# Writes of the gate tables and loads of the expert inputs moved from SyncE's DMA queue to ScalarE's

## The chip, the cores and the metric

The kernel runs on one core of a Trainium2 chip. The metric is the device time of one execution in microseconds (us): 3339.67 us before the change, the median of 3 runs (3336.93 to 3353.06).

## The reference, cut to what matters

One layer of a decoder, for 1024 prompt positions and 8 x 4 sample positions (1056 tokens, D = 1024): a mixing stage (RWKV-7 heads and pooling heads), then a layer of product-key experts, then a gate by a per-layer embedding and a final norm. The expert layer picks 8 x 16 of 16384 single-neuron experts for each token:

```python
q = (xb @ wq).reshape(PEER_BLOCK, PEER_HEADS, 2, PEER_DK_HALF)
s1 = jnp.einsum('thc,nc->thn', q[:, :, 0], sub_keys[0])
s2 = jnp.einsum('thc,nc->thn', q[:, :, 1], sub_keys[1])
v1, i1 = lax.top_k(s1, PEER_TOPK)
v2, i2 = lax.top_k(s2, PEER_TOPK)
cand = (v1[..., :, None] + v2[..., None, :])
sc, ci = lax.top_k(cand.reshape(...), PEER_TOPK)
expert = e1 * N_KEYS + e2
gate = jax.nn.softmax(sc)
act = gelu(einsum('thkd,td->thk', u_tab[expert], xb)) * gate
out = einsum('thk,thkd->td', act, v_tab[expert])
```

## The kernel before, in words

The work is one long program of unrolled instructions. A planner orders it: it takes the instructions as the code emits them, with their dependencies, and places them on the five engines by a model of their times. Each engine runs its own list in order. Almost every DMA is issued by SyncE (SP); the row gathers are issued by GpSimd (POOL). ScalarE (ACT) issues none.

Stages: `phase_a` projects and prepares the RWKV rows (0 to about 550 us). Then the tokens go in four groups (GROUPS, 288, 256, 256 and 256 tokens) through three streams that `merge` interleaves (lines 1124 to 1140): `b_stream` (the RWKV recurrence in chunks of 64 positions), `phase_c` (output projection, norm, query projection, key scores: its weights come as `whi`/`wlo` loads of 256 KB in `wblock`, lines 646 and 647, three buffers each), and `t_stream` (for the 672 tokens of positions GA to GB: top-k and gate tables, in `top` and `select`). Its scores go through memory as `sc_d` (written at line 747, read back at line 762).

The gate tables: for these 672 tokens the expert layer is computed densely, over all 16384 experts. `select` builds for 32 tokens at a time a table `gst` of 128 x 128 gates per token, as products of one-hot masks: VectorE and GpSimd build the masks `ab` (lines 898 to 900), TensorE multiplies them into PSUM (line 903), ScalarE copies the result into `gst` (line 905, 8 copies a table, 128 x 512 each), and the finished table (2 MB) is written to the memory tensor `g_d` (line 907). `gst` has two buffers. There are 21 such tables. `ugate` reads `g_d` back later, 32 loads `gq` of 1344 KB each, at line 1164.

The expert inputs: `phase_c` writes the normalised rows of the 672 tokens, split in two parts for precision, to `xh_d` and `xl_d` (line 719). When three of the four steps are emitted, the buffers of the recurrence are given up, and `XH` and `XL` are loaded into their place in 2 x 8 loads of 336 KB (lines 1148 and 1149). The dense stage (`dense`, `ublock`, `vblock`, with the matmuls in `emm` at line 1110) multiplies them with all expert rows: `eraw` loads of 512 KB at line 1084, split by ScalarE (`ehi`, line 1086) and by VectorE or GpSimd (`elo`, line 1088). It begins with `upre` at about 1215 us and runs to about 3200 us. Tokens beyond GB are done by row gathers on GpSimd and VectorE (lines 1210 to 1250) beside it.

In the code a DMA's issuing engine is the one named in the call: `nc.sync.dma_start` is SyncE, `nc.scalar.dma_start` ScalarE.

Of the kernel before, what the change touches and what calls it, by code (L numbers as in the profile page):

```python
# [10 lines left out]
F32 = mybir.dt.float32  # L11
# [30 lines left out]
GA, GB = 0, 672  # L42
# [4 lines left out]
TC = 32  # L47
# [3 lines left out]
GQ = 4  # L51
# [11 lines left out]
def body(ctx, tc, io):  # L63
    nc = tc.nc
# [12 lines left out]
    xh_d = dram.tile([128, KB, ND], F32, name="xh_d")  # L77
    xl_d = dram.tile([128, KB, ND], F32, name="xl_d")
# [4 lines left out]
    g_d = dram.tile([EB // GQ, 128, NTC, GQ, TC], F32, name="g_d")  # L83

    def v3(ap, n):
        return ap.rearrange("p (a b) -> p a b", b=n)
# [40 lines left out]
    def PS(tag):  # L127
        return pools[tag].tile([128, 512], F32, name="ps", tag="bc" if tag in ("b0", "b1") else tag)
# [620 lines left out]
    def top(tk, pos, mt):  # L749
        src = sc_d[TIDX[pos]]  # L750
        if mt > TC:
            m, nh, loads = mt, HEADS, [(slice(0, mt), 0)]
        else:
            m, nh = mt * SH, HEADS // SH
            loads = [(slice(g * mt, (g + 1) * mt), 2 * nh * g) for g in range(SH)]
        V12 = tk.tile([128, HEADS, 2, TOPK], F32, name="V12", bufs=1)
        I12 = tk.tile([128, HEADS, 2, TOPK], U32, name="I12", bufs=1)
        for i in range(2 * nh):
            if i % 4 == 0:
                sq = tk.tile([128, 4, 128], F32, name="scq", bufs=2)  # L760
                for d, j in loads:
                    nc.sync.dma_start(sq[d], src[:mt, j + i:j + i + 4, :])
            s_ = sq[:m, i % 4, :]
            v8, i8 = V12[:m, i // 2, i % 2, :], I12[:m, i // 2, i % 2, :]
            nc.vector.max(v8[:, 0:8], s_)
            nc.vector.max_index(i8[:, 0:8], v8[:, 0:8], s_)  # L766
            s2 = tk.tile([128, 128], F32, name="s2", bufs=2)
            nc.vector.match_replace(s2[:m], v8[:, 0:8], s_, -BIG)  # L768
            nc.vector.max(v8[:, 8:16], s2[:m])
            nc.vector.max_index(i8[:, 8:16], v8[:, 8:16], s2[:m])  # L770
            yield
        yield from select(tk, pos, mt, m, nh, V12, I12)


    def select(tk, col, mt, m, nh, V12, I12):
# [6 lines left out]
        for src, dst, add in ((V12, cand, TT), (F12, code, PTT)):  # L782
            off = 0
            for a, b, w in SEG:
                k = b - a
# [101 lines left out]
        for t1 in range(0, m, TC):  # L887
            st = gp.tile([128, EB, TC], F32, name="gst", bufs=2)
            for t2 in range(0, TC, 4):
                ps = PS("b3")  # L890
                t = t1 + t2
                ab = gp.tile([128, 6, EB, 2], F16, name="ab", bufs=3)

                def pairs(j, n):
                    e = e16[:, t // 4, j:j + n // 2].rearrange("p j (a b) -> p (j a) b", b=2)
                    return e[:, :, None, :].to_broadcast([128, n, EB, 2])

                TT(ab[:, 0:4], iota16[:, None, :, :].to_broadcast([128, 4, EB, 2]), pairs(0, 4), op=ALU.is_equal)  # L898
                TT(ab[:, 4:6], ab[:, 2:4], pairs(2, 2), op=ALU.mult)  # L899
                GLO(t)(ab[:, 2:4], ab[:, 2:4], pairs(3, 2), op=ALU.mult)  # L900
                for i in range(4):
                    for k in (4, 2):
                        mm(ps[:, i * 128:(i + 1) * 128], ab[:, k + i // 2, :, i % 2], ab[:, i // 2, :, i % 2],  # L903
                           start=k == 4, stop=k == 2)
                ACT(st[:, :, t2:t2 + 4].rearrange("p e t -> p t e"), v3(ps, 128), AF.Copy, scale=1.0 / GS)  # L905
                yield
            nc.sync.dma_start(g_d[:, :, (col + t1 - GA) // TC].rearrange("g p e t -> p g e t"), st.rearrange("p (g e) t -> p g e t", e=GQ))

    NG = len(GROUPS)
    NSLOT = 3  # L910
# [4 lines left out]
    def b_stream(ca, cb, ahead=2):  # L915
        while nxt[0] < cb or any(c < cb for c, _ in active):
            c = nxt[0]
            if (c < min(cb + ahead, NCH) and len(active) < NSLOT and (not active or since[0] >= STAG)
                    and not (held[0] and c % NSLOT == 1)):
                active.append((c, bchunk(c)))  # L920
                nxt[0], since[0] = c + 1, 0
            since[0] += 1
            for a in list(active):
                try:
                    next(a[1])
                except StopIteration:
                    active.remove(a)
                yield

    def b_len(ca, cb):  # L930
        return (cb - ca) * 19
# [6 lines left out]
    def t_stream(gi):  # L938
        for t0, m in tiles_of(gi):
            if GA <= GROUPS[gi][0] + t0 < GB:  # L940
                yield from top(tk, GROUPS[gi][0] + t0, m)

    def t_len(gi):
        n = 0
        for t0, m in tiles_of(gi):
            if GA <= GROUPS[gi][0] + t0 < GB:
                n += 24 + m // 4
        return n

    def merge(streams):  # L950
        live = [[0, n, g] for n, g in streams]
        while live:
            s = min(live, key=lambda s: s[0] / s[1])
            try:
                next(s[2])
                s[0] += 1
            except StopIteration:
                live.remove(s)
# [109 lines left out]
    def GLO(t):  # L1068
        return PTT if t % 12 else TT

    def xsplit():
        return (dr.tile([128, KB, ND], F32R, name="XH"), dr.tile([128, KB, ND], F32R, name="XL"))
# [45 lines left out]
    def upre():  # L1118
        for b in range(NPRE):
            ublock(b, PTT)  # L1120
            yield

    CL = [0, 24, 24, 24, 24]
    for step in range(1, NG + 1):
        streams = []
        if step < NG:
            c_ = BC[step + 2:step + 4]
            streams.append((b_len(*c_), b_stream(*c_)))
        if 0 <= step - 2 < NG:
            streams.append((t_len(step - 2), t_stream(step - 2)))  # L1130
        if 0 <= step - 1 < NG:
            streams.append((CL[step], phase_c(step - 1)))
        if step == NG:
            for _ in streams[0][1]:
                pass
            gstack.close()
            late = ctx.enter_context(tc.tile_pool(name="late", bufs=1, side="right", reuse_waits="tile"))
            gqp = ctx.enter_context(tc.tile_pool(name="gqp", bufs=2, side="right", reuse_waits="tile"))
            streams = [streams[1], (NPRE, upre())]
        merge(streams)  # L1140
        if step == NG - 1:
            nc.sync.dma_start(io["wkv_p"], S[-1])
            pbx.close()
            dr = ctx.enter_context(tc.tile_pool(name="dr", bufs=1, side="right", reuse_waits="tile"))
            dps = ctx.enter_context(tc.tile_pool(name="dps", bufs=2, side="right", space=bass.MemoryType.PSUM, reuse_waits="tile"))
            XH, XL = xsplit()
            for k in range(KB):
                nc.sync.dma_start(XH[:, k, :].bitcast(F32), xh_d[:, k, :])
                nc.sync.dma_start(XL[:, k, :].bitcast(F32), xl_d[:, k, :])
            xs = [(XH[:, k, :], XL[:, k, :]) for k in range(KB)]  # L1150
    def gtop(col):
        for _ in top(tk, GB + col, min(128, GT - col)):
# [170 lines left out]
    XH, XL = xsplit()  # L1323
# [71 lines left out]
def program(arrays, extra=()):  # L1395
    nc = bacc.Bacc("TRN2", target_bir_lowering=False, num_devices=1)
    io = {k: nc.dram_tensor(k, v.shape, mybir.dt.from_np(v.dtype), kind="ExternalInput").ap()
          for k, v in arrays.items()}
    for k, s in list(OUTS.items()) + list(extra):
        io[k] = nc.dram_tensor(k, s, F32, kind="ExternalOutput").ap()  # L1400
    with tile.TileContext(nc, schedule_with_timeline_sim=True) as tc, ExitStack() as ctx:
        body(ctx, tc, io)
    return nc
# [15 lines left out]
```

## Time and profile before

| | |
|---|---|
| median of the runs | 3339.67 us (3336.93 to 3353.06, 3 runs) |
| the profiled execution, its own time | 3365.37 us |
| its span, first to last instruction | 3363.7 us |
| TensorE (PE) busy in the span | 3145.6 us, 94% |
| VectorE (DVE) | 2585.2 us, 77% |
| ScalarE (ACT) | 1128.8 us, 34% |
| GpSimd (POOL) | 1736.5 us, 52% |
| mean granted TensorE clock | 0.968 |
| DMA queue q1 (all issues of SyncE) | 337952 packets, 472.91 MB |
| DMA queue q0 (the row gathers) | 110592 packets, 402.70 MB |
| gate tables written | 21 x 2048 KB |
| `XH` and `XL` loaded | 16 x 336 KB |

How to read it: busy times are those of one profiled execution, whose own time is 0.8% above the median of the runs. A DMA issue is not counted as busy time of its engine. In the order of time of SP, the second column is the time that the issue took on the queue; the transfer itself goes on behind it. L907 is line 907 of the kernel.

### The profile page before, as it was taken

Reading aid. Unit: us, or ns where it says so; the run is one execution under the profiler, and the core shown is the slowest. Engines: PE = TensorE matmul, PEld = TensorE weight load, DVE = VectorE, ACT = ScalarE, POOL = GpSimd, SP = SyncE. Lnnn points to the kernel's source line nnn. Section 1 sums busy time; section 2 is a strip of 40 time slices with the busy share of each in tenths; the row PEclk is TensorE's granted clock in tenths of the full one; section 3 lists DMA queues with packets and bytes.
Section 4 is the critical chain, followed back from the end, with each engine's and each line's share of the span. In section 5 each row is a group of like instructions: output and inputs, shape, how many; then the busy total and the mean of one; then the engine's idle time right before and its main releaser. Section 6 shows DMA issues by size and latency. Waiting matters only on the chain.

```text
span 3363.7 us, 66962 instructions
## 1 busy us (share of the span) xinstructions
PE 3145.6 (94%) x26777; PEld 3006.4 (89%) x26777; DVE 2585.2 (77%) x5124; ACT 1128.8 (34%) x1734; POOL 1736.5 (52%) x1439
## 2 busy tenths in 40 slices
PE   8997799896998988899999999999999999999997
PEld 7886688786787877899999999999999999999997
DVE  6766322229799879899898888888889888888966
ACT  6452322223555555431221222222222222222243
POOL 5433232215446455327666665566566566666634
PEclk9998899997999989999999999999999999999998
DMA  4668544665776796739999999999999999999933
GB/s 160 203 219 195 145 130 127 204 191 149 235 217 201 232 317 204 244 109 371 343 330 332 343 349 328 333 334 339 337 336 349 326 330 342 338 329 337 323 107 127
DMA packets 448856, 879.89 MB, mean 262 GB/s; under 512 B 110240, under 2 KB 233376, under 8 KB 444064
## 3 DMA queue, kind: packets, MB, share of 16 engines
q1 hardware_dynamic: 337952, 472.91, 43.8%
q0 software_dynamic: 110592, 402.70, 32.9%
q8 instruction: 210, 3.44, 0.4%
q14 instruction: 102, 0.84, 0.1%
HBM read 754.89 MB, written 120.60 MB: 260 GB/s over the span
## 4 chain that ended last, share of the span: by engine, by line
PE 54%; DVE 7%; DMA 2%; issue 1%; ACT 0%; POOL 0%; SPq 0%; ACTq 0%; DVEq 0%; POOLq 0%
PE pd L1110 53%; DVE ab L898 1%; DMA row<-u,idx 1%; DVE elo L1088 1%; DVE oh L850 0%; DMA scq<-sc_d 0%; DMA eraw<-wq 0%; DVE OT L1316 0%; DVE ab L899 0%; DVE I L766 0%; DVE s L768 0%; DVE tg L1302 0%; DVE I L770 0%; DMA g_d<-gst 0%; DMA gq<-g_d 0%
## 5 line engine op out<-in xcount | busy, mean ns | idle before, releaser
L1219 POOL DMA_INDIRECT row<-v,idx x384 | 530.6, 1382 | 330.8 <-DVE po L1236 150.9
L1219 POOL DMA_INDIRECT row<-u,idx x384 | 542.5, 1413 | 274.9 <-DVE row L1227 107.4
L1086 ACT ACTIVATE ehi<-eraw 128x1024 fp32r<-128x1024 f32 x278 | 294.5, 1060 | 1095.9 <-PE pd L1110 976.8
L1110 PE MATMUL pd<-XH,elo 128*128 128x336 f32 x2176 | 515.3, 318 | 5.9 <-POOL elo L125 4.7
L1110 PE MATMUL pd<-XL,ehi 128*128 128x336 f32 x2176 | 515.1, 317 | 0.0
L1110 PE MATMUL pd<-XH,ehi 128*128 128x336 f32 x2176 | 512.4, 316 | 0.4 <-ACT ehi L1086 0.4
L1110 PE MATMUL pd<-wh,ehi 128*128 128x336 f32 (+1 forms) x2112 | 504.1, 317 | 6.6 <-DVE tg L1300 6.2
L1110 PE MATMUL pd<-wl,ehi 128*128 128x336 f32 (+1 forms) x2112 | 504.0, 317 | 0.0
L1110 PE MATMUL pd<-wh,elo 128*128 128x336 f32 (+1 forms) x2112 | 503.9, 317 | 0.2 <-DVE elo L1088 0.2
L1236 DVE SCALAR_TENSOR_TENSOR po<-row,act,po 128x1024 f32<-128x1024 f32 x381 | 488.5, 1282 | 6.8
L1227 DVE SCALAR_TENSOR_TENSOR row<-row,xt 128x1024 f32<-128x1024 f32 x384 | 455.7, 1219 | 9.7 <-DMA row<-u,idx 9.5
L1110 PEld LDWEIGHTS pd<-XH,elo 128*128 128x128 f32 x2176 | 373.5, 188 | 7.1 <-POOL elo L125 5.5
L1088 DVE TENSOR_TENSOR elo<-eraw,ehi 128x1024 fp32r<-128x1024 f32 x256 | 318.3, 1243 | 77.2 <-ACT ehi L1086 69.0
L1110 PEld LDWEIGHTS pd<-XH,ehi 128*128 128x128 f32 x2176 | 372.9, 189 | 0.9 <-ACT ehi L1086 0.6
L1110 PEld LDWEIGHTS pd<-XL,ehi 128*128 128x128 f32 x2176 | 371.3, 188 | 0.2
L1110 PEld LDWEIGHTS pd<-wh,ehi 128*128 128x128 f32 x2112 | 362.6, 188 | 7.6 <-issue 7.4
L1110 PEld LDWEIGHTS pd<-wh,elo 128*128 128x128 f32 x2112 | 362.7, 188 | 0.6 <-DVE elo L1088 0.5
L1110 PEld LDWEIGHTS pd<-wl,ehi 128*128 128x128 f32 x2112 | 362.8, 188 | 0.0
L125 POOL TENSOR_TENSOR ab<-ab,e 128x512 f16<-128x512 f16 x110 | 130.1, 1185 | 180.6 <-DVE ab L899 139.0
L657 PE MATMUL ps<-hi,whi 128*128 128x256 f32 (+1 forms) x592 | 185.7, 315 | 29.3 <-DMA whi<-wc_d 15.8
L1179 DVE TENSOR_TENSOR OT<-pd,OT 128x672 f32<-128x672 f32 x120 | 102.9, 857 | 140.7 <-PE pd L1110 139.8
L905 ACT ACTIVATE gst<-ps 128x512 f32<-128x512 f32 x168 | 174.9, 1089 | 85.5 <-PE ps L903 78.4
(428 smaller groups left out, 5526.9 us busy)
## 6 DMA issues: line engine op xcount, KB each, us to landing
eraw<-uT SPq DMA_DIRECT2D x128, 512.0 KB
eraw<-vP SPq DMA_DIRECT2D x128, 512.0 KB
g_d<-gst SPq DMA_DIRECT2D x21, 2048.0 KB
gq<-g_d SPq DMA_DIRECT2D x32, 1344.0 KB
whi<-wc_d SPq DMA_DIRECT2D x148, 256.0 KB
wlo<-wc_d SPq DMA_DIRECT2D x148, 256.0 KB
fdc<-fd SPq DMA_DIRECT2D x16, 896.0 KB
wc_d<-shi SPq DMA_DIRECT2D x40, 256.0 KB
```

Source lines behind the costliest of these rows:

```text
L125: nc.gpsimd.tensor_tensor(out, a, b, op=op)
L657: mm(ps[:, :n], whi[:, kk, :], xhi[:, k, :n], start=k == 0, stop=False)
L898: TT(ab[:, 0:4], iota16[:, None, :, :].to_broadcast([128, 4, EB, 2]), pairs(0, 4), op=ALU.is_equal)
L905: ACT(st[:, :, t2:t2 + 4].rearrange("p e t -> p t e"), v3(ps, 128), AF.Copy, scale=1.0 / GS)
L1086: ACT(hi, raw, AF.Copy)
L1088: sub(lo, raw, hi.bitcast(F32), op=ALU.subtract)
L1110: mm(ps[:, a, :n], w_[:, k, :], x_[:, s:s + n], start=first, stop=last)
L1179: TT(halves(OT[db]), ps[:, :, :NH], halves(OT[db]), op=ALU.add)
L1219: nc.gpsimd.indirect_dma_start(out=r[:m], out_offset=None, in_=io[tab], in_offset=bass.IndirectOffsetOnAxis(ap=idx[:m, hh, k:k + 1], axis=0))
L1227: STT(r[:m], r[:m], 1.0, xt[:m], op0=ALU.mult, op1=ALU.mult, accum_out=pre[:m, k:k + 1])
L1236: STT(po[:m], r[:m], act[:m, k:k + 1], po[:m], op0=ALU.mult, op1=ALU.add)
```

## The change

The 21 writes of the gate tables and the 16 loads of `XH` and `XL` are issued by ScalarE instead of SyncE. Nothing else differs: sizes, buffers and dependencies are the same.

```diff
-            nc.sync.dma_start(g_d[:, :, (col + t1 - GA) // TC].rearrange("g p e t -> p g e t"), st.rearrange("p (g e) t -> p g e t", e=GQ))
+            nc.scalar.dma_start(g_d[:, :, (col + t1 - GA) // TC].rearrange("g p e t -> p g e t"), st.rearrange("p (g e) t -> p g e t", e=GQ))
...
             for k in range(KB):
-                nc.sync.dma_start(XH[:, k, :].bitcast(F32), xh_d[:, k, :])
-                nc.sync.dma_start(XL[:, k, :].bitcast(F32), xl_d[:, k, :])
+                nc.scalar.dma_start(XH[:, k, :].bitcast(F32), xh_d[:, k, :])
+                nc.scalar.dma_start(XL[:, k, :].bitcast(F32), xl_d[:, k, :])
```

## Rows read from the trace of the kernel before

**Rows 1.** The chain that ended last, 1540 us to the end: start, us, what

```profile
1548.60 518.04 PE pd L1110 x3372
...
2643.67 560.14 PE pd L1110 x3644
```

**Rows 2.** Busy time of each engine by stage (clock, DMA share, GB/s last)

```profile
800.00:1400.00 600.00, 519.61 (x6117) 462.14 (x6113) 520.53 (x1971) 307.81 (x489) 300.55 (x311) 0.92 0.75 230
1400.00:1550.00 150.00, 147.65 (x963) 146.85 (x964) 134.08 (x546) 54.13 (x75) 52.67 (x57) 1.00 0.54 191
```

**Rows 3.** Waits of PE, 800 to 1400 us: us in total, times, longest

```profile
PE ps L903 <- DVE ab L899: 30.7, 21, 4.2
PE ps L657 <- DMA whi<-wc_d: 9.1, 7, 2.2
PE ps L903 <- ACT gst L905: 7.9, 14, 1.5
...
PE ps L659 <- DMA wlo<-wc_d: 1.4, 3, 0.8
```

**Rows 4.** Wait of DVE, 800 to 1400 us

```profile
DVE V L765 <- DMA scq<-sc_d: 7.6, 5, 3.6
```

**Rows 5.** SP in order of time: start, us of the issue, engine, line

```profile
835.74 0.37 SPq L907 DMA_DIRECT2D g_d<-gst  x1
836.20 5.95 SPq L647 DMA_DIRECT2D wlo<-wc_d  x1
...
856.33 3.42 SPq L907 DMA_DIRECT2D g_d<-gst  x1
...
1183.24 0.37 SPq L907 DMA_DIRECT2D g_d<-gst  x1
1183.85 8.97 SPq L646 DMA_DIRECT2D whi<-wc_d  x1
...
1207.43 0.38 SPq L907 DMA_DIRECT2D g_d<-gst  x1
1208.04 9.27 SPq L646 DMA_DIRECT2D whi<-wc_d  x1
...
1356.70 4.79 SPq L646 DMA_DIRECT2D whi<-wc_d  x1
```

**Rows 6.** PE in order of time, the larger waits for these loads (in brackets)

```profile
910.65 0.39 PE L657 MATMUL ps<-hi,whi 128*128 128x256 f32 x1 [0.54 <-DMA whi<-wc_d]
...
958.11 0.39 PE L657 MATMUL ps<-hi,whi 128*128 128x256 f32 x1 [1.07 <-DMA whi<-wc_d]
...
959.77 0.38 PE L659 MATMUL ps<-hi,wlo 128*128 128x256 f32 x1 [0.39 <-DMA wlo<-wc_d]
...
1094.19 0.38 PE L657 MATMUL ps<-hi,whi 128*128 128x256 f32 x1 [1.22 <-DMA whi<-wc_d]
...
1116.46 0.39 PE L659 MATMUL ps<-hi,wlo 128*128 128x256 f32 x1 [0.81 <-DMA wlo<-wc_d]
...
1157.50 0.58 PE L657 MATMUL ps<-hi,whi 128*128 128x256 f32 x1 [2.17 <-DMA whi<-wc_d]
```

**Rows 7.** PE's wait before the first dense block (order of time)

```profile
1221.01 0.93 PE L1110 MATMUL pd<-XH,elo 128*128 128x336 f32 x2 [4.68 <-POOL elo L125]
```

**Rows 8.** The issues of XH and XL: ns least, median, most; first and last start

```profile
L1148 SPq DMA_DIRECT2D XH<-xh_d x8: 319/372/653, 1176.3 to 1199.6; - x8
...
L1149 SPq DMA_DIRECT2D XL<-xl_d x8: 320/374/708, 1178.0 to 1200.5; - x8
```

**Rows 9.** The row gathers issued by POOL, ns least, median, most

```profile
L1219 POOL DMA_INDIRECT row<-u,idx x384: 932/1598/1992, 1507.2 to 3149.9; - x192
```

**Rows 10.** ACT, copies of L905 in 800 to 1400 us: busy, mean ns, idle before

```profile
L905 ACT ACTIVATE gst<-ps 128x512 f32<-128x512 f32 x168 | 174.9, 1089 | 85.5 <-PE ps L903 78.4 <-DMA g_d<-gst 5.3 <-ACT cF L827 0.4
```

**Rows 11.** The last table's write, in the chain of 1250 to 1560 us

```profile
1374.75 7.94 DMA g_d<-gst
...
1385.78 11.28 DMA eraw<-wq
```

## The prediction

> **What bounds the kernel now.** I read four views, in this order. First the chain of work that ended last: from 1548 us to the end it is TensorE's dense matmuls with hardly a break [rows 1]. Its three long pieces, the first of 518 us and the last of 560 us, need no explanation beyond TensorE itself, and none of the moved DMAs runs there. Whatever the change gives, it must give before 1548 us, by letting that chain start earlier, and what it gives there arrives at the end nearly whole, since the chain behind it is unbroken.
>
> Second, the busy time by stage. All 21 table writes and all 16 loads of XH and XL fall between 800 and 1400 us. There PE is busy for 519.6 of 600 us at a mean granted clock of 0.92, DVE for 520.5, ACT for 307.8 [rows 2]. So PE is idle for 80.4 us, and that is the pool from which a gain can be drawn. In the next 150 us PE is idle for 2.4 us, at full clock. DVE is as loaded as PE in the stage: a wait taken from PE may turn into a wait for DVE.
>
> Third, what PE waits for in these 600 us [rows 3]. The largest item is DVE's masks, 30.7 us, which the change doesn't touch. The weight loads of the projection (whi, wlo) cost 9.1 + 1.4 = 10.5 us in ten waits, ScalarE's copy of the table 7.9 us in 14.
>
> Fourth, SP in order of time [rows 5]. A table write itself takes 0.37 us on the queue. But the DMA issue behind it takes 5.95 us the first time, 4.79 us behind the second to last, against 0.37 us in the median for loads of a like size [rows 8]. I added up the next issue behind each of 20 of the 21 writes (the last has nothing close behind it): 108 us, from 1.7 to 9.3 us each; less 20 x 0.37 us that is about 100 us in which SP stands behind a table. That is what the change is aimed at, and the question is how little of it reaches PE.
>
> **The change part by part.**
>
> *The 21 writes leave SP.* The loads queued behind them no longer wait. Of the ten waits of PE for whi and wlo, six are for loads that stood behind a write: 0.54, 1.07, 0.39, 1.22, 0.81 and 2.17 us [rows 6], together 6.2 us. The other four, 10.5 - 6.2 = 4.3 us, have no table ahead of their load. The remaining 94 of the 100 us are hidden already: three buffers of weights are loaded ahead, and PE has other streams' matmuls to do. So this term is -6.2 us. Its ends: 0 if the loads are then just as late because the same 2 MB is moving beside them, and -10.5 us if all such waits go. I take 6.2, since a 256 KB load then has to share the transfer time with the table rather than stand behind the whole of it. The Trainium skill has a rule against this term (DMA: Bandwidth & Descriptors, Issuing engines are not separate DMA queues): DMAs from several engines end on the same 16 DMA engines, and issuing from more than one saves only the time of issuing, usually small beside the transfer. By that rule the term is 0 and the sum below +0.6 us; the row differs in that the issuing time was 100 us here. Freeing SP also lets the scores come back sooner: DVE waits 7.6 us for scq [rows 4]. Idle time of DVE doesn't delay PE's chain by itself, and no wait in rows 3 names the top-k; 0 here, -7.6 as the far end.
>
> *The 16 loads leave SP.* Their issues take 0.37 us in the median [rows 8], about 6 us of SP between 1176 and 1201 us. No instruction waits for XH or XL: PE's first wait in the dense stage, 4.7 us, is for elo on POOL [rows 7]. Cost and gain 0; what hides it is the eraw load and its split, which end later.
>
> *ScalarE gets 37 issues.* No row shows an issue on ACT. The nearest is SP's, 0.37 us [rows 5, 8]; the far one is POOL's issue of a gather, 1.6 us in the median [rows 9]. That is 14 us of ACT's time or 59 us, beside 307.8 us of work in 600. I take 0.37 us, as the transfers are of SP's kind. Each table write stands right behind the copy that finishes the table, so what is queued behind it on ACT is the next copy out of PSUM or a split, for which PE waits. PE waits 7.9 us for these copies against 174.9 us of their busy time [rows 3, 10], a share of 4.5%: 14 us of issuing puts +0.6 us on the path. If the cover were gone the ends are +14 and, by POOL's price, +59 us.
>
> *Waits that move to ACT.* A table write waits for its own copy, which has just ended on the same engine: nothing new. An XH load waits until the recurrence has given up its buffers, and holds ACT's later work if that comes late; on SP the sixteen issues took at most 0.71 us each, so 0. What can hold ACT for longer is an issue that meets a busy queue: once a table write itself took 3.42 us [rows 5]. That one is a rival below.
>
> *The last table.* Its write takes 7.94 us to land and the first gq load waits for it [rows 11]; that is the same from either queue: 0.
>
> *The planner's order.* Moving 37 issues can shift where it places other instructions. No row shows it; I bound it by the largest single wait of PE in the stage, 4.7 us [rows 7], to either side, and take 0.
>
> **The sum**: -6.2 + 0.6 = -5.6 us against the profiled execution (3365.37 us, its span 3363.7): 3359.8 us. The median of the runs is 25.7 us lower, with the same program; the rows don't show where it lies, so I carry the difference over: 3339.7 - 5.6 = 3334 us.
>
> What this kernel's measurement can tell from no change is about 0.5%, 16.7 us: faster is below 3323 us, slower above 3356 us.
>
> **The rivals.**
>
> *A larger gain: the stage tightens.* SP is freed for 100 us, and what comes sooner isn't only weights. If all waits of PE for weights go (10.5 us), DVE's waits for scores too (7.6 us), and PE, with fewer gaps, is granted a clock of 0.93 instead of 0.92 (519.6 x 0.01 / 0.93 = 5.6 us), it is 24 us: 3316 us. For it: the clock is 1.00 right behind the stage, where PE has no gaps [rows 2]. Against it: the 30.7 us for DVE's masks stay.
>
> *Slower: ScalarE is held behind its own tables.* Between 1176 and 1201 us the XH and XL loads and the tables come together, and there the issue behind a table took 8.97 us and 9.27 us on SP [rows 5]. On ACT the issue behind a table is an XH load or the next table. If it is held there, no PSUM bank is emptied for 9 us and PE stops. Two such holds, 18.2 us, less the 5.6 us gained, is +12.6 us and can't be told. The point from which it decides is the third hold: 3 x 9.1 - 5.6 = +22 us, 3362 us. For it: the transfers are the same and 16 loads come within 25 us. Against it: the XH and XL issues on SP took 0.71 us at most [rows 8], so a weight load stood in the held place, and the planner may put other work there again.
>
> *Nothing moves: the issues of both engines meet in the same place.* Then SP's loads still stand behind a table that ACT has issued, -6.2 becomes 0, and +0.6 is left: 3340 us, at worst +14 us, 3354 us. In the profile all plain DMAs are in one queue, so no row speaks for or against. The rule of the Trainium skill named above would bring this rival about. The same page of the Trainium skill (DMA: Bandwidth & Descriptors, Queues, rings and completion order) says that each DMA engine takes turns between the two queues; by that rule a load would pass the table, which is the forecast.
>
> **How the numbers follow.** The forecast has 0.47, the larger gain 0.25, nothing 0.15, the hold 0.13. Faster by over 0.5%: most of the larger gain, 0.23, and 0.04 of the forecast, 0.27. Slower: 0.11 of the hold and 0.01 each of the forecast and of nothing, 0.13. Within 0.5%: 0.60. The range reaches to the larger gain and 4 us past it (the planner's bound), and up to where nothing is at its worst (3354 us) plus the same 4 us: 3312 to 3358 us; the hold from its third on and gains beyond 28 us are left out.
>
> **What would show it.** Right: a second plain queue in the profile with some 50 MB (21 x 2048 KB + 16 x 336 KB); SP's issues behind a table at 0.4 us; PE's waits for whi and wlo near 4 us; ACT's issues near 0.4 us; PE's idle time between 800 and 1400 us down from 80 to about 75. The larger gain: the clock above 0.92 there. The hold: ACT issues of several us at lines 907 or 1148. Nothing: SP still held for 5 us behind a table. The forecast is wrong if the dense chain starts more than 17 us earlier or later than at 1548 us.

## The result and the profile after

The change makes the kernel slower: a median of 3363.28 us (3359.87 to 3369.04, 6 runs) against 3344.05 us (3336.93 to 3353.06, 6 runs) for the kernel before on the same chip. The ratio is 1.0054, with a 95% interval of 1.0035 to 1.0072, so the loss is 18 us and lies between 12 and 24. I had forecast 3334 us and given 3358 us as the upper end.

One thing is to be known before two spans are compared. The profiled execution of before that the prediction rests on was one of its slowest (span 3363.7 us), and that of after is one of its fastest (span 3358.5 us). So I took a second profile of the kernel before (the last experiment below, span 3348.5 us), and stages are compared with both.

The dense chain, which answers to [rows 1], starts 3.4 us earlier than in the first profile of before, 1545.17 us against 1548.60. Between two executions this says little: the two profiles of before are 11.5 us apart at the write of line 1142 already (1163.3 and 1151.8 us). The stage of the change says more. The busy times of after, by stage (the columns are those of [rows 2]: stretch, length, then PE, its weight loads, DVE, ACT and POOL, the granted clock, the DMA share, GB/s):

```profile
800.00:1400.00 600.00, 511.38 (x6036) 459.84 (x6036) 517.83 (x1906) 306.21 (x489) 301.53 (x307) 0.93 0.73 229
1400.00:1550.00 150.00, 143.98 (x919) 142.85 (x918) 135.01 (x543) 50.31 (x68) 51.35 (x56) 0.99 0.55 200
```

and of the second profile of before:

```profile
800.00:1400.00 600.00, 523.00 (x6115) 468.26 (x6116) 521.13 (x1948) 313.57 (x500) 298.07 (x308) 0.93 0.76 237
```

PE is busy for 511.4 us where before had 519.6 [rows 2] and 523.0: it stands idle for 8 to 12 us more, at the same clock. The waits of PE in that stage, after (us in total, times, longest), answer to [rows 3]:

```profile
PE ps L903 <- ACT gst L905: 20.2, 8, 12.8
PE ps L903 <- DVE ab L899: 16.7, 12, 5.5
PE ps L657 <- DMA whi<-wc_d: 8.9, 6, 3.4
PE ps L659 <- DMA wlo<-wc_d: 3.0, 4, 1.2
```

Two readings. The waits for weights, which the change was aimed at, are not shorter: 8.9 + 3.0 = 11.9 us against 10.5 [rows 3] (10.1 in the second profile). And the wait for ScalarE's copies has grown from 7.9 us in 14 to 20.2 us in 8, of which a single one is 12.8 us. That one stop is the place to look at. The matmul that ends it, in PE's order of time in after:

```profile
1174.50 1.64 PE L903 MATMUL ps<-ab 128*128 128x128 f16 x15
1188.96 1.16 PE L903 MATMUL ps<-ab 128*128 128x128 f16 x9 [12.82 <-ACT gst L905]
```

and what ScalarE did in that time (ACTq is a DMA issue on ScalarE; in brackets the idle time ahead of an instruction and what ended it):

```profile
1171.73 0.33 ACTq L1148 DMA_DIRECT2D XH<-xh_d  x1
1172.10 2.01 ACT L905 ACTIVATE gst<-ps 128x512 f32<-128x512 f32 x2 [2.50 <-DMA XH<-xh_d]
...
1177.30 0.38 ACTq L907 DMA_DIRECT2D g_d<-gst  x1
1177.72 0.39 ACT L738 ACTIVATE q<-ps 128x256 f32<-128x256 f32 x1 [3.61 <-DMA eraw<-uT]
1180.81 7.03 ACTq L1149 DMA_DIRECT2D XL<-xl_d  x1
1187.88 1.02 ACT L905 ACTIVATE gst<-ps 128x512 f32<-128x512 f32 x1 [9.78 <-issue]
```

ScalarE issues a table at 1177.30 us, and the next load, XL, takes 7.03 us to issue behind it. The copy of line 905 stands behind that issue in ScalarE's list, ScalarE empties no PSUM bank from 1178.11 to 1187.88 us (9.78 us), and PE, which needs one, stops for 12.82 us. Note also the other two brackets: a copy of `gst` reads no `XH`, and a copy of `q` no `eraw`. Where the releaser of an instruction is a tile that it does not read, it is not its own wait that ended, but that of the DMA issue ahead of it in the same list.

On SP most of the hold is gone, as forecast. The issues of the weights in that stage of after (ns least, median, most; first and last start):

```profile
L646 SPq DMA_DIRECT2D whi<-wc_d x97: 319/320/4001, 814.1 to 1345.0; - x97
...
L647 SPq DMA_DIRECT2D wlo<-wc_d x97: 319/387/2247, 815.7 to 1351.8; - x97
```

The longest are 4.0 and 2.2 us, where before had 9.27 [rows 5]. And the queues of after (packets, MB, share) show that the change does what it says:

```profile
q1 hardware_dynamic: 249296, 423.36, 38.3%
...
q10 hardware_dynamic: 88656, 49.55, 4.8%
```

### The profile page after: what moved, and what is told of

It reads as the page before. It is cut to its first block, busy times and chain, and to the rows that moved or that the text cites. A ratio compares the mean times of both kernels' runs of the same rounds, so it can differ in the third digit from the quotient of the medians.

```text
span 3358.5 us, 66936 instructions
## 1 busy us (share of the span) xinstructions
PE 3136.9 (93%) x26777; PEld 3002.6 (89%) x26777; DVE 2596.3 (77%) x5124; ACT 1130.5 (34%) x1734; POOL 1747.7 (52%) x1439
## 4 chain that ended last, share of the span: by engine, by line
PE 66%; DVE 15%; DMA 6%; POOL 2%; issue 2%; ACT 2%; SPq 0%; ACTq 0%; DVEq 0%; POOLq 0%
PE pd L1110 53%; PE ps L486 5%; PE ps L657 2%; DVE ab L898 2%; PE ps L659 2%; PE ps L658 2%; DVE ab L899 1%; DMA sraw<-wq 1%; PE ps L903 1%; DMA whi<-wc_d 1%; DMA wlo<-wc_d 1%; DMA g_d<-gst 1%; DVE I L766 1%; DVE oh L850 1%; PE ps L1014 1%
## 5 line engine op out<-in xcount | busy, mean ns | idle before, releaser
L1219 POOL DMA_INDIRECT row<-v,idx x384 | 538.9, 1403 | 314.0 <-DVE po L1236 138.4
L905 ACT ACTIVATE gst<-ps 128x512 f32<-128x512 f32 x168 | 177.1, 1097 | 119.4 <-PE ps L903 98.1
```

What stands on the lines that cost most here:

```text
L1219: nc.gpsimd.indirect_dma_start(out=r[:m], out_offset=None, in_=io[tab], in_offset=bass.IndirectOffsetOnAxis(ap=idx[:m, hh, k:k + 1], axis=0))
```

## The experiments

**Theories.** The expectations name them by number. 1: the planner's new order costs the time. 2: the second queue costs it by sharing the transfer engines, whoever issues. 3a: ScalarE is held at a DMA issue until an older transfer has landed, and what stands behind the issue in its list is what PE needs. 3b: it is held only by an issue right behind a table of its own, as in the rival of the prediction. In the first runs, theory 3 is a narrower thing: the loads of XH and XL alone hold ScalarE. In the last runs, theory A is 3a, B is 2, and C that SP, freed of tables, brings weights earlier.

**Order or queue.** The change moves instructions as well as queues, since the planner sees other costs. To part the two I pinned the order of every engine's instructions, with dependencies that carry no wait, to the one the planner finds for a given choice of queues, and then issued the DMAs from others (in angle brackets, what differs between the runs).

```diff
-            nc.sync.dma_start(g_d[:, :, (col + t1 - GA) // TC]...
+            QT(nc).dma_start(g_d[:, :, (col + t1 - GA) // TC]...
...
+    QUEUES[:] = <queues whose order is taken>
+    order = [i.name for b in program(arrays).m.functions[0].blocks for i in b.instructions]
+    QUEUES[:] = <queues that issue>
+    nc = program(arrays, order=order)
```

Before's order, all 37 DMAs on ScalarE:

> Every engine's order is held to the one of the kernel before; only the 37 DMAs are issued by ScalarE. If the planner's new order costs the time (theory 1), this is not slower than before: 3338 to 3345 us, 0.998 to 1.000 of it. If issuing on ScalarE or the way the transfers then share the DMA engines costs it (theory 2), it is as slow as the change: 3360 us or more, 1.005.

After's order, all 37 on SP:

> Every engine's order is held to the one of the changed kernel, but all DMAs are issued by SyncE again. Theory 1 (order): as slow as the change or slower, 3360 to 3370 us, 1.005 to 1.008. Theory 2 (queue): as before, 3344 us, 1.000.

Measured: 1.0045 (1.0027 to 1.0063) for the queue alone, 0.9998 (0.9984 to 1.0011) for the order alone. Theory 1 falls: the loss belongs to the queue. ScalarE with the queue alone:

```profile
1173.77 0.38 ACTq L907 DMA_DIRECT2D g_d<-gst  x1
1174.19 7.84 ACTq L1149 DMA_DIRECT2D XL<-xl_d  x1
...
1182.63 0.38 ACT L738 ACTIVATE q<-ps 128x256 f32<-128x256 f32 x1 [8.89 <-issue]
```

It is the same picture in another order: 7.84 us behind a table, 8.89 us of nothing on ScalarE. PE's longest stop behind `gst` is 6.7 us there, and its waits for `gst` sum to 22.5 us. With after's order and SP's queue PE is busy in the stage as before, so after's 511.4 us are not its order's:

```profile
800.00:1400.00 600.00, 523.06 (x6150) 468.20 (x6149) 528.26 (x1962) 310.34 (x494) 301.23 (x309) 0.93 0.75 229
```

**Tables or inputs, the planner free.** Only line 907 on ScalarE, and only lines 1148 and 1149:

```diff
-            nc.sync.dma_start(g_d[:, :, (col + t1 - GA) // TC]...
+            nc.scalar.dma_start(g_d[:, :, (col + t1 - GA) // TC]...
```

> Only the 21 table writes go to ScalarE, the planner is free. Theory 1: a third order, so any value from 3335 to 3370 us, not the sum of parts. Theory 2: most of the 19 us, as 44 of the 50 MB move, about 3358 us. Theory 3 (the XH and XL loads hold ScalarE for 7 us each time): as before or faster, 3338 to 3344 us.

> Only the 16 loads of XH and XL go to ScalarE, the planner is free. Theory 1: any value from 3335 to 3370 us. Theory 2: little, 3344 to 3348 us. Theory 3: nearly all of the 19 us, 3360 us.

Measured: tables 1.0012 (1.0002 to 1.0021), inputs 1.0061 (1.0045 to 1.0077). With the tables alone, PE's waits for whi and wlo are:

```profile
PE ps L657 <- DMA whi<-wc_d: 5.8, 6, 2.1
PE ps L659 <- DMA wlo<-wc_d: 5.1, 4, 1.9
```

Together that is 10.9 us: SP's queue is rid of all 21 tables and PE waits as long as before (10.5 and 10.1 us). That holds for the order of this run; with before's order pinned (the runs below) the same sum is 6.2 us with the 21 tables on ScalarE and 8.0 us with 17 of them, 2 to 4 us less. PE has its one large stop here too:

```profile
1208.31 1.89 PE L903 MATMUL ps<-ab 128*128 128x128 f16 x16 [10.21 <-ACT gst L905]
```

That a stop of 10.2 us goes with a loss of only 4 us (0.12%) in this run is not explained; the order here is one that I have not timed by itself. With the inputs alone the stop stands at the head of the dense stage, where PE waits 8.78 us for ScalarE's split `ehi`, and the waits for whi and wlo are 13.8 + 3.5 = 17.3 us from 800 to 1400 us, so that run has more in it than the hold.

**Tables or inputs, in before's order.** So I did the same two with before's order pinned.

> Order of the kernel before on every engine; only the 21 table writes are issued by ScalarE. If the loads of XH and XL are the whole loss (theory 3), the tables cost nothing: 1.000 of before, at best 0.998 if SP's freed 100 us still reach PE. If the tables on ScalarE have a price of their own (theory 2), 1.002 or more.

> Order of the kernel before on every engine; only the 16 loads of XH and XL are issued by ScalarE, the tables stay on SyncE. If ScalarE is held by each load until an older transfer has landed (theory 3a), this alone is slower by what the whole change costs in this order, 1.0045. If it is held only where a load stands behind a table on ScalarE's own queue (theory 3b, the 7 us at 1181 us), no such place is left and it is 1.000 to 1.001.

Measured: 1.0049 (1.0031 to 1.0067) and 1.0049 (1.0031 to 1.0066). Each half costs as much as the whole (1.0045), so the two do not add up: either suffices to stop PE in that stretch. Theory 3 as first put, the loads alone, falls here: it gave the tables 1.000. With the tables alone on ScalarE, ScalarE:

```profile
1196.18 0.37 ACTq L907 DMA_DIRECT2D g_d<-gst  x1
1196.65 1.02 ACT L905 ACTIVATE gst<-ps 128x512 f32<-128x512 f32 x1 [12.21 <-DMA XL<-xl_d]
```

and PE:

```profile
1197.72 0.27 PE L903 MATMUL ps<-ab 128*128 128x128 f16 x1 [12.06 <-ACT gst L905]
```

Here nothing is slow behind a table. The table's own issue takes 0.37 us, but stands for 12.21 us until an XL load has landed, which SP issued. With the inputs alone on ScalarE there is no table in its queue at all, and ScalarE shows:

```profile
1185.07 0.33 ACTq L1148 DMA_DIRECT2D XH<-xh_d  x1
1185.44 1.02 ACT L905 ACTIVATE gst<-ps 128x512 f32<-128x512 f32 x1 [9.94 <-DMA whi<-wc_d]
```

An XH load stands until a weight load of SP has landed, and PE's next matmul of line 903 (1186.51 us) has waited 7.51 us. Theory 3b alone can't give that; 3a can.

**Why an issue waits for another engine's transfer** is seen in the compiled program. Each DMA issued by SP or ScalarE counts its completion on one of eight counters, which the two queues share, and waits, besides its data, for the older DMA of its counter. A few of the DMAs of the run with four tables (below), in program order: what they wait for (engine counts, DMA counters), and the counter that they raise, by 16:

```
SP          [('DMAHW4', 1328)]                      raises DMAHW4  XH load
SP          [('DMAHW5', 1328)]                      raises DMAHW5  XL load, the last
...
Activation  [('Activation', 927), ('DMAHW5', 1344)] raises DMAHW5  the 15th table
```

The 15th table waits for its own copy (Activation 927), and for the last XL load (DMAHW5 at 1328 + 16).

**The number of loads.** XH and XL by one DMA each (2 loads of 2688 KB), and in halves (32 loads of 168 KB):

```diff
-            for k in range(KB):
-                nc.sync.dma_start(XH[:, k, :].bitcast(F32), xh_d[:, k, :])
...
+            nc.scalar.dma_start(XH.bitcast(F32), xh_d)
```

```diff
+            for k, o in ((k, o) for k in range(KB) for o in (0, NH)):
+                nc.scalar.dma_start(XH[:, k, o:o + NH].bitcast(F32), xh_d[:, k, o:o + NH])
```

> The change, but XH and XL are loaded by one DMA each (2 instead of 16 issues, the same bytes). Theory 3a (a hold per issue): most of the loss goes, 1.000 to 1.002. If the place of the transfer among the others costs it, not the number of issues: as the change, 1.005. The first dense matmul then waits for the whole XH, which may cost some us of its own.

> The change with 32 loads of half the size (168 KB each). Theory 3a: about twice the holds, 1.008 to 1.011. Theory 3b or the place of the transfer: as the change, 1.005.

Measured: 1.0033 (1.0022 to 1.0043) with 2 loads, 1.0054 with 16 (the change), 1.0067 (1.0048 to 1.0086) with 32. Neither came out as 3a had forecast, 1.000 to 1.002 for 2 loads and 1.008 to 1.011 for 32; the interval for 32 holds 3a's lower end as well as 3b's 1.005. The medians rise with the number of issues, but 16 and 32 can't be told apart, so these runs show no price for each issue. With 32, PE stops twice:

```profile
1191.58 1.14 PE L903 MATMUL ps<-ab 128*128 128x128 f16 x9 [11.32 <-ACT gst L905]
...
1212.40 1.89 PE L903 MATMUL ps<-ab 128*128 128x128 f16 x16 [8.53 <-ACT gst L905]
```

With two, it is not ScalarE that stops PE, but a weight load that was issued behind the two large ones; from 1140 to 1190 us loads of `whi` took 6.1 us to land in the median, and 16.8 at most:

```profile
1174.58 0.58 PE L657 MATMUL ps<-hi,whi 128*128 128x256 f32 x1 [14.60 <-DMA whi<-wc_d]
```

So the 2-load run doesn't measure the hold; I read what is left there as theory 2's part in its worst form.

**Where the issue stands.** The last runs test 3a by place. Before's order; first all tables on ScalarE but the four of the crowded stretch (the 13th to the 16th), then only these four, then the sixteen inputs on GpSimd (POOL), whose DMAs have eight counters of their own in the compiled program.

```diff
-    return getattr(nc, QUEUES[0])
+    return nc.scalar if table in QUEUES[0] else nc.sync
...
+    QUEUES[:] = (*range(12), *range(16, 21)), "sync"
...
+    QUEUES[:] = (12, 13, 14, 15), "sync"
...
+    QUEUES[:] = (), "gpsimd"
```

> Before's order on every engine; 17 of the 21 tables issued by ScalarE, but the four whose writes fall in or beside the stretch of 1150 to 1250 us (the 13th to the 16th), and all sixteen input loads, by SP. Theory A (ScalarE is held at an issue until an older transfer has landed, and that is long only where the DMA engines are full): 0.999 to 1.001, PE busy for 39 to 41 of the 50 us of 1150 to 1200, as in the kernel before. Theory B (every table on the second queue costs its share of the 0.5% that all 21 cost): 1.004. Rival C (SP freed of tables brings the expert weights earlier): 0.998.

> The converse: before's order, and only the 13th to the 16th table issued by ScalarE, the other 17 and all inputs by SP. Theory A: nearly all of the loss of the 21 tables, 1.003 to 1.005, with one stop of PE of 8 to 13 us behind ScalarE's gst between 1170 and 1210 us. Theory B: four twenty-firsts of it, 1.001.

> Before's order, tables on SP, and the sixteen input loads issued by POOL, whose DMAs have completion counters of their own in the compiled program, so that an issue there waits for fewer older transfers and ScalarE issues none. Theory A: 0.998 to 1.002, no PE stop of over 5 us behind ScalarE's gst between 1150 and 1210 us. Theory B (the sharing of the DMA engines by loads that start earlier, whoever issues them): 1.004 or more, with PE as idle in 1150 to 1200 us as in the run with the inputs on ScalarE (20 us of 50).

> The kernel before, unchanged, for a second profile: PE busy for 39 to 41 of the 50 us of 1150 to 1200, as in its first profile, by every theory; a value near 30 would say that the stop is in the spread of one kernel's executions.

Measured: 17 tables away from the stretch 1.0003 (0.9992 to 1.0015); the four tables in it 1.0035 (1.0021 to 1.0048); inputs on POOL 1.0014 (1.0004 to 1.0024). Four tables cost what 21 cost within the intervals, and the other 17 cost nothing. That is 3a's forecast, and not that of a charge for each table. ScalarE with the four tables:

```profile
1200.58 0.37 ACTq L907 DMA_DIRECT2D g_d<-gst  x1
1201.05 1.02 ACT L905 ACTIVATE gst<-ps 128x512 f32<-128x512 f32 x1 [10.67 <-DMA XL<-xl_d]
```

This is the 15th table of the list above, held for the last XL load, and PE's stop behind it:

```profile
1202.12 0.27 PE L903 MATMUL ps<-ab 128*128 128x128 f16 x1 [10.51 <-ACT gst L905]
```

With those four on SP instead, it is SP that is held, twice:

```profile
1169.51 8.55 SPq L646 DMA_DIRECT2D whi<-wc_d  x1
...
1193.13 9.49 SPq L646 DMA_DIRECT2D whi<-wc_d  x1
```

8.55 and 9.49 us, as long as any hold on ScalarE, and the time is before's. A hold costs what stands behind it: on SP other loads, which come early; on ScalarE the copies that PE waits for.

PE's busy time from 1150 to 1200 us, for the second profile of before, for after, for the 17 tables, for the four, and for POOL, in that order, one fence for each kernel:

```profile
1150.00:1200.00 50.00, 38.88 (x395) 35.48 (x392) 35.99 (x87) 25.77 (x33) 16.68 (x15) 0.88 0.91 312
```

```profile
1150.00:1200.00 50.00, 29.73 (x262) 27.70 (x262) 26.25 (x66) 18.79 (x23) 16.05 (x12) 0.76 0.90 306
```

```profile
1150.00:1200.00 50.00, 38.32 (x359) 34.36 (x358) 37.03 (x88) 28.13 (x36) 18.02 (x16) 0.85 0.95 325
```

```profile
1150.00:1200.00 50.00, 31.64 (x302) 28.27 (x299) 28.83 (x77) 17.48 (x23) 14.58 (x13) 0.83 0.84 278
```

```profile
1150.00:1200.00 50.00, 37.19 (x376) 34.02 (x373) 30.31 (x79) 20.92 (x28) 22.71 (x29) 0.90 0.90 320
```

PE loses some 7 to 9 us in these 50 wherever ScalarE is held, and DVE, which waits for PE, about as much; the DMA share is 0.84 to 0.95 in all five. The granted clock of these 50 us, the third number from the end, is 0.88 in both profiles of before, 0.76 in after and 0.83 with the four tables, so the work that PE does falls by more than its busy time (395 matmuls, 262 and 302); over the whole stage it is 0.92 or 0.93 in all of these. The two profiles of before speak against a mere spread between executions: the first has 40.26 us here, the second 38.88, and 38.88 and the 38.32 of the 17 tables lie just under the 39 to 41 that I had expected. With the inputs on POOL the large stop is absent (its longest wait for gst from 1100 to 1260 us is 1.6 us). PE's waits for weights from 1100 to 1260 us there:

```profile
PE ps L657 <- DMA whi<-wc_d: 7.5, 4, 2.4
...
PE ps L659 <- DMA wlo<-wc_d: 2.7, 3, 1.7
```

Together 10.2 us, against 3.7 + 0.9 = 4.6 us in the second profile of before. So theory 2 seems to have a part too: sixteen loads that no longer stand in SP's list crowd the weights, and that can make up the 0.14% (5 us) that POOL's version loses. No run parts it from the masks `ab` that POOL builds behind its sixteen issues. It is the smaller part: the same sixteen loads on ScalarE lose 0.49%.

**The size, from two landmarks.** Two issues of SP stand at either end of the stretch, in all kernels with before's order: the write of the RWKV state (line 1142) and the first read of a finished table (line 1164). Second profile of before (the two times at the end are the first and the last start):

```profile
L1142 SPq DMA_DIRECT2D wkv_p<-S x1: 337/337/337, 1151.8 to 1151.8; - x1
...
L1164 SPq DMA_DIRECT2D gq<-g_d x32: 319/327/1099, 1369.2 to 3050.6; - x32
```

The four tables on ScalarE:

```profile
L1142 SPq DMA_DIRECT2D wkv_p<-S x1: 338/338/338, 1155.4 to 1155.4; - x1
...
L1164 SPq DMA_DIRECT2D gq<-g_d x32: 320/326/942, 1385.5 to 3068.7; - x32
```

The difference is 1369.2 - 1151.8 = 217.4 us and 1385.5 - 1155.4 = 230.1 us: 12.7 us longer. In the same way:

| before's order | line 1142 to line 1164, us | ratio |
|---|---|---|
| before, two profiles | 219.4, 217.4 | 1 |
| 17 tables on ScalarE | 217.2 | 1.0003 |
| four tables | 230.1 | 1.0035 |
| 21 tables | 230.1 | 1.0049 |
| all 37 | 231.9 | 1.0045 |
| 16 inputs on ScalarE | 235.1 | 1.0049 |
| 16 inputs on POOL | 227.5 | 1.0014 |

Those on ScalarE that touch the crowded stretch lose 11 to 18 us of it, and 0.35% to 0.49% of 3350 us is 12 to 16 us: the stretch holds the loss. POOL's profiled execution lost some 9 us there, more than its median of eleven runs shows.

The first landmark is itself an issue that waits, and not equally long: in the second profile of before SP has passed one semaphore of it at 1146.1 us and issues it at 1151.8, with the four tables at 1155.3 and 1155.4. So these lengths are good to some 6 us. DVE's list gives a finer count: in all kernels with before's order DVE starts the same 6157 instructions, in the same order but for some neighbours. Between its instructions that start at 1160 and at 1210 us in the second profile of before, DVE falls back against that profile by 14.6 us with the four tables, 13.6 with 21, 16.2 with all 37, 15.9 with the inputs on ScalarE, 7.9 with them on POOL and 0.0 with the 17 tables; in the first profile of before it is 0.3. From there to the end no kernel moves by more than 4.4 us either way. In the same way, between the instructions at 1160 and 1200 us, after falls back by 9.8 us against the run with its own order on SP's queue. No version tried beats the kernel before; that with 17 tables on ScalarE equals it.

## Why the prediction was wrong

The failing step is **"Waits that move to ACT"**, where I put both kinds of DMA at nothing: a table write waits for its own copy, "nothing new", and of the loads "on SP the sixteen issues took at most 0.71 us each, so 0". It measured some 10 to 12 us: PE's wait for `gst` grew by 10 to 12 us, nearly all in one stop, and PE's busy time in the stage fell by 11.7 us against the run with after's order on SP's queue (523.06 - 511.38). For the tables, "nothing new" was false: in before's order a table's issue stood until an XL load of SP had landed, with ScalarE idle for 12.21 us (21 tables) and 10.67 us (four). For the loads there are two mistakes. I took the time of an issue for the whole of its cost; an issue that waits for an older transfer shows as idle time *ahead* of it, which on SP nobody counts and on ScalarE stands in front of a copy. And I priced the sixteen loads by where they stood on SP, which had whole weight loads in the held places. In after, ScalarE was idle for 2.50, 3.61 and 9.78 us behind issues within 20 us. PE waited 1.86 us behind the first; the end of the second and the whole of the third lie in its stop of 12.82 us.

**"The 21 writes leave SP": -6.2 us, measured 0 in time.** SP's hold did shrink (9.27 us down to at most 4.0). PE's waits for weights fell by less than I took: from 9.6 + 3.6 = 13.2 us in the run with after's order on SP's queue to 11.9 in after, and from 10.5 and 10.1 us to 5.3 + 2.7 = 8.0 with 17 tables away and 4.7 + 1.5 = 6.2 with 21. And none of it shows in the time: the 17 tables, which no large stop hides, measured 1.0003 (0.9992 to 1.0015), where the first five of my six waits, 4.0 us, would be 0.9988 (the sixth stood behind the 13th table, which is not among these). So the end that I had named, 0, was right. The rule that I had set against the term, of the Trainium skill (DMA: Bandwidth & Descriptors, Issuing engines are not separate DMA queues), says that a second issuing engine saves only issue time. For this half the runs agree: with the 17 tables away SP's issues in the stage took 199.5 us instead of 253.3, and the kernel was no faster.

**The other terms** held. "ScalarE gets 37 issues": 0.33 to 0.44 us each in after but for two (0.76 and the 7.03), as taken; its +0.6 us is not measured by itself. The planner's order: 0, measured 0.9998. Scores: DVE waits 7.8 us for scq in after against 7.6 [rows 4], 0. The last table: 9.10 us to land against 7.94 [rows 11], 1 us.

**The rivals.** "ScalarE is held behind its own tables" had the right engine, the right stretch (1176 to 1201 us) and the right price of a hold (8.9 to 9.8 us behind a table in after and in the run with the queue alone), and its 3362 us came within 2 us of the median. That nearness is luck: the sum was three holds less a gain, from a median of 3339.7 us. What ran was one long stop and no gain, from a median of 3344.05. And tables in ScalarE's own queue aren't needed: inputs alone on ScalarE lose as much, at the counters. My reason against it, that the XH and XL issues on SP took 0.71 us at most, is the failing step again. "Nothing moves" had the gain right, at 0, but not its reason: SP's issues hardly stand any more. The range ends at 3358 us because I left the hold, from its third on, out of it. The median lies 5.3 us above that, of which 4.4 us is before itself, 3344.05 us over 6 runs and not 3339.67 over 3; the direction was wrong in any case, 5.6 us faster forecast and 18 us slower measured.

What stays open: the two landmarks in after are 242.8 us apart, 10.5 us more than with the same order on SP's queue (232.3), and the ratio says 12 to 24 us; the few us between are not located. In after's hold the slow issue behind the table takes 7.03 of the 9.78 us and the wait ahead of it 2.7 (1178.11 to 1180.81 us); I tried no kernel that has the one without the other there. A kernel in which ScalarE's DMAs have counters of their own was not tried.

## What to carry to other kernels

Before a DMA is moved to a compute engine, read what stands behind it in that engine's list, and ask not what the issue takes but which older transfers it must wait for, and how long a transfer takes to land in that stretch. A hold on a queue that carries only loads may be free; the same hold ahead of a PSUM copy is a stop of TensorE. If it must be, move the ones that lie where the DMA engines are not full, and look for rows whose releaser is a tile that the instruction doesn't read.

## What was not expected of the hardware and the program

- Holds of two kinds look different in the trace: behind a table in the same queue the *next issue itself* takes long (7.03 and 7.84 us on ScalarE, 8.55 and 9.49 us on SP), while a wait on a shared counter leaves the issue at 0.33 to 0.37 us and shows as idle time of the engine (10.67 and 12.21 us; 9.94 us with the inputs alone, where two issues share it).
- The queues of SP and ScalarE are not independent in this program: the eight completion counters are shared, so that an engine can be held by a transfer that another engine issued.
- An issue of a 336 KB load takes 0.54 us on POOL and 0.33 us on ScalarE, by the medians of the two runs that moved the inputs alone in before's order; I had bounded ScalarE's by POOL's gathers, 1.6 us [rows 9].
